# FFN gate and up products as Strassen's seven products of 2x2 blocks (over pairs of f tiles, pairs of k tiles and token halves)

## The chip, the core and the metric

The kernel runs on one core of a Trainium2 chip. The time is that of one execution on the device, in microseconds (us); the time before is the median of 3 runs. In the texts PE is TensorE (its weight loads are PEld), DVE is VectorE, ACT is ScalarE, POOL is GpSimd, and SP is SyncE, on whose queue the kernel issues all its DMAs. L191 is line 191 of the kernel before.

## The reference, cut to what matters

One step of a two-layer streaming encoder in float32. There are T = 640 tokens (512 of one new stream and 8 x 16 of running streams), and each has D = 1024 channels. The stages, in order, are: FFN 0a, the mLSTM and SSD mixer ("ab"), FFN 0b, FFN 1a, the gated DeltaNet mixer ("gdn"), FFN 1b, and a last norm. The change is in the FFNs:

```python
D_MODEL = 1024
D_FF = 2816
def swiglu(x, w_gate, w_up, w_down):
    return (jax.nn.silu(x @ w_gate) * (x @ w_up)) @ w_down
...
    x = x + 0.5 * swiglu(rmsnorm(x, norm_g[l, 0]), ffn_w_gate[l, 0], ffn_w_up[l, 0], ffn_w_down[l, 0])
```

## The kernel before, in words

**Layout.** Activations lie by channels: `self.x[d]`, d = 0..7, is a tile of 128 channels by 640 tokens. A float32 product is made of three float32r products. Both operands are split exactly into a high and a low part, and hi x hi, hi x lo and lo x hi are summed in PSUM (`passes`).

**Activations.** `prep(d)` runs for each channel tile as soon as its residual is written. ACT writes the high part of x times the norm's gain (L273), DVE the low part (L274), and both add the tile's squares to the norm's sum (`sumsq`: ACT L265, DVE L266). The norm's factor itself is needed only behind the products. `rstd` computes it with a small PE product of that sum (L295), a chain of short DVE instructions (L297, L284 to L289), and a second PE product (L307) that spreads it over the partitions as `R` (L308, L309).

**Weights.** `wload` brings [128, 8, 256] of a weight (1 MB) into one of two buffers `wraw` (gate, down and mixer weights) or of two buffers `wraw2` (up weights); line 148 issues the DMA. `split` then works in units of 512 columns: ACT copies the high part (L174), and POOL subtracts it from the weight to give the low part (L175). The results lie in eight buffers `wsp`, so four units (pairs of high and low) can be ready or in use. Splitting has a higher priority in the scheduler than the work around it (`AHEAD` = 300), so it runs as far ahead of PE as `wsp` allows.

**Products.** `mmT` makes one [128 x 640] output in PSUM from 8 k tiles. For each k tile it makes the three passes, and for each pass the two token halves of 320. These are 48 matmuls of 128 x 128 by 128 x 320, all on L191, each with its own weight load. PSUM has two tiles `big` of two banks each, and four tiles `small` of one bank.

**An FFN.** `ffn` goes over 22 f tiles of 128 in three groups, `FF_GROUPS = ((0, 8), (8, 15), (15, 22))`. For each f tile it makes the gate product and the up product, each into one `big`. DVE multiplies each by R (L336), ACT applies silu (L338), DVE multiplies gate by up (L339), and ACT and DVE split the result into h (L341, L342). After each group `wout` adds the group's share of the down product to x. It goes over eight output tiles j, two to each load, and each j takes one `big`; the two alternate, so that the eviction of one (L367, or L365 where the scale is 1) lies beside the products of the other. In the last group of a stage `wout` calls the next stage's `prep` after each j. The last group of FFN 1b goes through `finish` instead (L1701 and behind), which also makes the last norm and writes the output.

**Mixers.** Their projections use `mmT` and `projR` (L386), and their output products use `wout` with two h-like tiles at a time (`out2`, 8 calls in ab and 4 in gdn). Their recurrences are Python generators that advance one step at each `tick`; `mmT` ticks once for each k tile. Where the main stream needs a generator's result, `until` ticks with no main work beside it.

**Order of the work.** The program is written out in full, and a scheduler orders each engine's queue ahead of time by priority and by its own estimate of when inputs are ready. At run time every queue goes in that order.

## Time and profile before

| | |
|---|---|
| time, median of 3 runs (lowest, highest) | 3054.94 us (3054.13, 3055.04) |
| span of the profiled execution | 3055.5 us |
| mean granted TensorE clock | 0.989 |
| PE busy; PEld busy | 2992.0 us; 2889.9 us |
| DVE; ACT; POOL busy | 1219.9; 1090.0; 1038.7 us |
| matmuls on L191, gate, up and mixer projections | 10560 |

A row that groups instructions gives line, engine, operation, written <- read tile, shape, count, then busy time in us, mean ns of one, and the engine's idle time just before them with what ended it. A row of the timeline gives start, length (both in us), engine, line and operation. A row of the windows gives a stretch from:to in us, its length, each engine's busy time with the number of instructions, the granted clock, the DMA share and GB/s. The profiled execution's span is 0.6 us above the median of the runs.

### The profile page before, as it was taken

The page shows a single profiled execution, that of the slowest core. Times are in us where ns is not written, and L with a number is a line of the kernel's source. Part 1 is how long each engine was busy: PE and PEld are TensorE (multiplying, and loading weights), DVE is VectorE, ACT ScalarE, POOL GpSimd, SP SyncE. Part 2 cuts the span into 40 slices and gives each one's busy share as a digit, 9 for nine tenths or more (in the row PEclk, how much of TensorE's full clock was granted, in tenths as well). Part 3 has the DMA queues.
Part 4 walks back from the last instruction along what each step waited for, and adds up shares of the span by engine and source line. Part 5 has one row for each costly group of instructions (what it writes and reads, how often), then busy time and mean ns, then how long its engine had stood idle before and what let it go on. Part 6 is the DMA issues. An engine that isn't in the chain of part 4 may idle for free. (4 is left out here: it accounts for less than half of the span.)

```text
span 3055.5 us, 50975 instructions
## 1 busy us (share of the span) xinstructions
PE 2992.0 (98%) x20870; PEld 2889.9 (95%) x20870; DVE 1219.9 (40%) x2419; ACT 1090.0 (36%) x2385; POOL 1038.7 (34%) x871
## 2 busy tenths in 40 slices
PE   8999999999999999999999999999999999999998
PEld 8999999999988899999999999999888998999998
DVE  4212125233566662121233122236777755212124
ACT  4222234343444342222232222234555454222225
POOL 3333332222223133333333333333323223333334
PEclk9999999999999999999999999999999999999999
DMA  5222213222313232222132222122122213222213
GB/s 149 70 69 66 94 37 83 72 81 88 96 56 91 71 115 70 69 82 78 53 95 70 84 70 74 58 75 61 48 73 56 86 51 108 71 68 82 79 52 107
DMA packets 268159, 233.70 MB, mean 76 GB/s; under 512 B 22103, under 2 KB 266468, under 8 KB 267926
## 3 DMA queue, kind: packets, MB, share of 16 engines
q1 hardware_dynamic: 267926, 230.44, 24.6%
q8 instruction: 165, 2.70, 0.4%
q14 instruction: 68, 0.56, 0.1%
HBM read 211.80 MB, written 18.60 MB: 75 GB/s over the span
## 5 line engine op out<-in xcount | busy, mean ns | idle before, releaser
L175 POOL TENSOR_TENSOR wsp<-wraw,wsp 128x512 fp32r<-128x512 f32 (+2 forms) x808 | 993.4, 1233 | 1970.0 <-ACT wsp L174 1786.3
L191 PE MATMUL big<-xg,wsp 128*128 128x320 f32 x10560 | 1609.3, 310 | 0.9 <-DVE x L252 0.9
L191 PEld LDWEIGHTS big<-xg,wsp 128*128 128x128 f32 x10560 | 1558.0, 188 | 22.5 <-issue 19.7
L174 ACT ACTIVATE wsp<-wraw 128x512 fp32r<-128x512 f32 (+2 forms) x808 | 480.1, 597 | 1292.0 <-PE big L191 1151.8
L191 PE MATMUL big<-h,wsp 128*128 128x320 f32 x3888 | 572.1, 308 | 0.0
L191 PEld LDWEIGHTS big<-h,wsp 128*128 128x128 f32 x3888 | 570.7, 188 | 0.0
L336 DVE TENSOR_TENSOR gu<-big,R 128x640 f32<-128x640 f32 x176 | 145.3, 826 | 817.9 <-PE big L191 817.6
L386 PE MATMUL big<-wsp,xg 128*128 128x256 f32 x1920 | 240.5, 282 | 1.5 <-DVE zs L1680 1.4
L367 DVE SCALAR_TENSOR_TENSOR x<-big,x 128x640 f32<-128x640 f32 x88 | 72.6, 825 | 410.9 <-PE big L191 410.9
L386 PEld LDWEIGHTS big<-wsp,xg 128*128 128x128 f32 x1920 | 229.3, 190 | 4.4 <-DVE zs L1680 2.2
L191 PE MATMUL big<-y,wsp 128*128 128x320 f32 x768 | 130.3, 318 | 5.0 <-DVE x L365 5.0
L339 DVE TENSOR_TENSOR gu<-gu,gu 128x640 f32<-128x640 f32 x88 | 129.7, 1474 | 9.4 <-DVE gu L336 0.5
L191 PEld LDWEIGHTS big<-y,wsp 128*128 128x128 f32 x768 | 114.4, 189 | 16.1 <-issue 14.7
L341 ACT ACTIVATE h<-gu 128x640 fp32r<-128x640 f32 x88 | 65.0, 739 | 179.7 <-DVE gu L339 179.7
L568 DVE SCALAR_TENSOR_TENSOR tmp<-tmp,taps,tmp 128x664 f32<-128x664 f32 x108 | 101.9, 943 | 14.4 <-ACT tmp L562 13.1
L342 DVE TENSOR_TENSOR h<-gu,h 128x640 fp32r<-128x640 f32 x88 | 72.8, 828 | 70.8 <-ACT h L341 70.8
L365 DVE TENSOR_TENSOR x<-big,x 128x640 f32<-128x640 f32 x96 | 78.4, 821 | 49.0 <-PE big L191 48.2
L338 ACT ACTIVATE gu<-gu 128x640 f32<-128x640 f32 x88 | 65.1, 740 | 39.0 <-DVE gu L336 38.9
L191 PE MATMUL big<-yT,wsp 128*128 128x320 f32 x384 | 70.9, 334 | 3.5 <-DVE x L365 2.7
L191 PEld LDWEIGHTS big<-yT,wsp 128*128 128x128 f32 x384 | 60.8, 201 | 10.5 <-issue 5.6
L274 DVE SCALAR_TENSOR_TENSOR xg<-x,gain,xg 128x640 fp32r<-128x640 f32 x48 | 48.8, 1023 | 28.4 <-ACT xg L273 28.3
L1701 PE MATMUL big<-h,wsp 128*128 128x384 f32 (+1 forms) x336 | 54.1, 314 | 0.4 <-DVE h L342 0.2
(426 smaller groups left out, 2089.6 us busy)
## 6 DMA issues: line engine op xcount, KB each, us to landing
wraw<-in_ffn_w_up SPq DMA_DIRECT2D x43, 1024.0 KB
wraw<-in_ffn_w_gate SPq DMA_DIRECT2D x43, 1024.0 KB
wraw<-in_ffn_w_down SPq DMA_DIRECT2D x36, 896.0 KB
wraw<-in_ffn_w_down SPq DMA_DIRECT2D x16, 1024.0 KB
wraw<-in_ab_w_in SPq DMA_DIRECT2D x16, 1024.0 KB
wraw<-in_gdn_w_in SPq DMA_DIRECT2D x16, 1024.0 KB
wraw<-in_ab_w_out SPq DMA_DIRECT2D x32, 256.0 KB
wraw<-in_ab_w_in SPq DMA_DIRECT2D x12, 512.0 KB
```

The costliest lines, as they stand in the source:

```text
L174: nc.scalar.activation(out=hi, in_=src[:, i : i + n], func=AF.Copy)
L175: nc.gpsimd.tensor_tensor(lo, src[:, i : i + n], hi.bitcast(F32), ALU.subtract)
L191: self.nc.tensor.matmul(ps[:, half, :HT], lhsT=wp, rhs=ap[:, half * HT : half * HT + HT], start=(k == 0 and i == 0), stop=(k == n - 1 and ...
L336: nc.vector.tensor_tensor(e.rearrange("p (a b) -> p a b", a=2), ps[:, :, :HT], self.r2(), ALU.mult)
L338: nc.scalar.activation(out=ev[0], in_=ev[0], func=AF.Silu)
L339: nc.vector.tensor_tensor(ev[0], ev[0], ev[1], ALU.mult)
L341: nc.scalar.activation(out=h[:, 0], in_=ev[0], func=AF.Copy)
L342: nc.vector.tensor_tensor(h[:, 1], ev[0], h[:, 0].bitcast(F32), ALU.subtract)
L365: nc.vector.tensor_tensor(xj, ps[:, :, :HT], xj, ALU.add)
L367: nc.vector.scalar_tensor_tensor(xj, ps[:, :, :HT], scale, xj, ALU.mult, ALU.add)
L386: self.nc.tensor.matmul(ps[:, t % 2, :256], lhsT=ap[:, t * P : (t + 1) * P], rhs=wp, start=(k == 0 and i == 0), stop=(k == ND - 1 and i == 2))
L568: nc.vector.scalar_tensor_tensor(y[:, :n], xp[:, k : k + n], taps[:, j, k : k + 1], y[:, :n], ALU.mult, ALU.add)
```

## The change

The gate and up products go over pairs. For two f tiles (columns of the weight), two k tiles and the two token halves, the eight block products are replaced by seven products (Strassen's, in Winograd's form) of sums of weight blocks with sums of activation blocks. One `pair_up` makes the gate (or the up) outputs of two f tiles: seven products, each over 4 pairs of k tiles and three passes. These are 84 matmuls of 128 x 128 by 128 x 320, where two calls of `mmT` made 96.

- **Weights** (`weights7`). Of the seven weight operands three are blocks as loaded and four are sums, made on DVE from 512-column blocks into five buffers `S`. All seven are split by ACT and POOL as before, in units of 512 columns.
- **Activations** (`prep2`, in place of `prep` ahead of an FFN). For every pair of channel tiles it makes the seven activation operands, each split into high and low, partly in buffers shared with the mixers (`ext` "A", "B", "C").
- **Results** (`pair_up`). The seven products are combined from four PSUM banks by DVE. The gate pair uses both `big`, the up pair all four `small`. Some banks are read while their sum is half made, and are added to afterwards.
- **h.** Silu, gate times up, and the split of h work on both f tiles at once (1280 columns).
- **`wout`** goes over two output tiles j together: k outside, j inside, both `big` at once, and one tick per k tile. It splits the weights of two j in one call.
- **Buffers.** `wraw2` has one buffer; h has three of twice the size; several mixer tiles take theirs from `ext`; `finish` takes its output rows from the tiles `xg`.
- **Groups.** `FF_GROUPS` has four groups, the last of six f tiles.

Comments and docstrings, dropped in the diff, are left out below, as are the mixers' lines that only take a tile from `ext`.

```diff
-FF_GROUPS = ((0, 8), (8, 15), (15, 22))
+FF_GROUPS = ((0, 4), (4, 10), (10, 16), (16, 22))
...
+    def ext(self, which, dtype=F32):
+        return lambda tag, shape, bufs=1: self.t(f"ext{which}", shape, {"A": 6, "B": 4, "C": 2}[which], dtype)
...
-        w = tile("wraw2", [P, 2048], bufs=2) if tile else self.t("wraw", [P, 2048], bufs=2)
+        w = tile("wraw2", [P, 2048]) if tile else self.t("wraw", [P, 2048], bufs=2)
...
+    def prep2(self, d, which, total=True):
+        nc = self.nc
+        if total:
+            self.sumsq(d)
+        if d % 2 == 0:
+            return
+        p = d // 2
+        x0, x1 = self.x[d - 1], self.x[d]
...
+        def gained(dst, src, g):
+            nc.scalar.activation(out=dst[:, 0], in_=src, func=AF.Copy, scale=g)
+            nc.vector.scalar_tensor_tensor(dst[:, 1], src, g, dst[:, 0].bitcast(F32), ALU.mult, ALU.subtract)
+        def plain(dst, src):
+            nc.scalar.activation(out=dst[:, 0], in_=src, func=AF.Copy)
+            nc.vector.tensor_tensor(dst[:, 1], src, dst[:, 0].bitcast(F32), ALU.subtract)
+        u, v = self.tmp(), self.tmp()
+        d0, d1, y, s2 = u[:, :HT], u[:, HT:T], v[:, :HT], v[:, HT:T]
+        gained(a[:, :, lo_half], x0[:, lo_half], g0)
+        nc.vector.tensor_tensor(d0, x0[:, hi_half], x0[:, lo_half], ALU.subtract)
+        nc.vector.tensor_tensor(d1, x1[:, lo_half], x1[:, hi_half], ALU.subtract)
+        nc.scalar.activation(out=d0, in_=d0, func=AF.Copy, scale=g0)
+        nc.vector.scalar_tensor_tensor(s2, x1[:, hi_half], g1, d0, ALU.mult, ALU.subtract)
+        plain(t2, s2)
+        plain(t1, d0)
+        nc.scalar.activation(out=y, in_=x0[:, hi_half], func=AF.Copy, scale=g0)
+        nc.vector.scalar_tensor_tensor(y, x1[:, hi_half], g1, y, ALU.mult, ALU.subtract)
+        plain(t3, y)
+        gained(b, x1, g1)
+        nc.vector.scalar_tensor_tensor(d1, d1, g1, d0, ALU.mult, ALU.add)
+        plain(t4, d1)
+        self.xs[p] = (a[:, :, lo_half], t2, t1, t3, b[:, :, lo_half], b[:, :, hi_half], t4)
...
+    def weights7(self, tile, raw):
...
+        def total(x, y, op):
+            s = tile("S", [P, ND // 2, P], bufs=5)
+            with self.tc.high_priority(offset=self.ahead):
+                nc.vector.tensor_tensor(s, x, y, op)
+            return s
+        def parts(src):
+            hi, lo = (self.unit().rearrange("p (a b) -> p a b", b=P) for _ in range(2))
+            with self.tc.high_priority(offset=self.ahead):
+                nc.scalar.activation(out=hi, in_=src, func=AF.Copy)
+                nc.gpsimd.tensor_tensor(lo, src, hi.bitcast(F32), ALU.subtract)
+            return hi, lo
+        yield parts(a11)
+        s1 = total(a21, a22, ALU.add)
+        s2 = total(s1, a11, ALU.subtract)
+        yield parts(s2)
+        yield parts(s1)
+        yield parts(total(a11, a21, ALU.subtract))
+        yield parts(a12)
+        yield parts(total(a12, s2, ALU.subtract))
+        yield parts(a22)
+    def product(self, ps, w, acts, first, last):
+        n = len(acts)
+        for k, a in enumerate(acts):
+            for i, (wp, ap) in enumerate(((w[0], 0), (w[0], 1), (w[1], 0))):
+                self.nc.tensor.matmul(ps, lhsT=wp[:, k], rhs=a[:, ap],
...
+    def pair_up(self, tile, raw, banks):
...
+        b1, b6, b5, b7 = banks
+        w = self.weights7(tile, raw)
+        B = list(zip(*self.xs))
+        self.product(b1, next(w), B[0], True, False)
+        self.product(b6, next(w), B[1], True, True)
+        nc.scalar.copy(u, b1)
+        nc.vector.tensor_tensor(u, b6, u, ALU.add)
+        self.product(b5, next(w), B[2], True, False)
+        nc.vector.tensor_tensor(v, b5, u, ALU.add)
+        self.product(b7, next(w), B[3], True, False)
+        nc.vector.tensor_tensor(c22, b7, v, ALU.add)
+        self.product(b1, next(w), B[4], False, True)
+        nc.vector.tensor_tensor(c11, b1, self.R[:, :HT], ALU.mult)
+        self.product(b5, next(w), B[5], False, True)
+        nc.vector.tensor_tensor(c12, b5, u, ALU.add)
+        self.product(b7, next(w), B[6], False, True)
+        nc.vector.tensor_tensor(c21, b7, u, ALU.add)
+        nc.vector.tensor_tensor(c12, c12, self.R[:, HT:], ALU.mult)
+        nc.vector.tensor_tensor(g[:, T:], g[:, T:], self.R, ALU.mult)
+        return g
...
-            for f in range(g0, g1):
+            for f in range(g0, g1, 2):
...
-                for n in ("g", "u"):
-                    w = self.split(raw[n][:, :, c : c + P], ND, P)
-                    ps = self.big()
-                    self.mmT(ps, w, self.xg)
-                    e = tile("gu", [P, T], bufs=4)
-                    nc.vector.tensor_tensor(e.rearrange("p (a b) -> p a b", a=2), ps[:, :, :HT], self.r2(), ALU.mult)
-                    ev.append(e)
+                ev = [self.pair_up(tile, r, self.banks(i == 0)) for i, r in enumerate(raw)]
                 nc.scalar.activation(out=ev[0], in_=ev[0], func=AF.Silu)
                 nc.vector.tensor_tensor(ev[0], ev[0], ev[1], ALU.mult)
...
         for jb in range(4):
             raw = self.wload(w[:, :, jb * 256 : jb * 256 + 256], n, 256)
-            for j in (2 * jb, 2 * jb + 1):
-                c = (j % 2) * P
-                wj = self.split(raw[:, :, c : c + P], n, P)
-                ps = self.big()
-                self.mmT(ps, wj, acts)
+            wj = self.split(raw, n, 256)
+            pss = [self.big(), self.big()]
+            for k, a in enumerate(acts):
+                for c, ps in enumerate(pss):
+                    for i, (wp, ap) in enumerate(self.passes(wj[k], a)):
+                        for half in range(2):
+                            nc.tensor.matmul(
...
+                self.tick()
+            for c, ps in enumerate(pss):
+                j = 2 * jb + c
...
-            return lambda d, total=True: self.prep(d, 3 * l + {"a": 0, "b": 2}.get(s, 1), total)
+            prep = self.prep2 if kind == "ffn" else self.prep
+            return lambda d, total=True: prep(d, 3 * l + {"a": 0, "b": 2}.get(s, 1), total)
```

More of the change, by code (lines that the diff above doesn't have):

```diff
@@ new lines, in product @@
+    def product(self, ps, w, acts, first, last):
+        n = len(acts)
+        for k, a in enumerate(acts):
+            for i, (wp, ap) in enumerate(((w[0], 0), (w[0], 1), (w[1], 0))):
+                self.nc.tensor.matmul(
+                    ps,
+                    lhsT=wp[:, k],
+                    rhs=a[:, ap],
+                    start=(first and k == 0 and i == 0),
+                    stop=(last and k == n - 1 and i == 2),
+                    skip_group_check=True,
+                )
@@ new lines, in banks @@
+    def banks(self, whole):
+        if whole:
+            a, b = self.big(), self.big()
+            return a[:, 0, :HT], a[:, 1, :HT], b[:, 0, :HT], b[:, 1, :HT]
+        return tuple(self.small()[:, :HT] for _ in range(4))
+    def pair_up(self, tile, raw, banks):
+        nc = self.nc
+        g = tile("G", [P, 2 * T], bufs=2)
+        c11, c12, c21, c22 = (g[:, i * HT : i * HT + HT] for i in range(4))
+        uv = tile("uv", [P, 2, HT], bufs=2)
+        u, v = uv[:, 0], uv[:, 1]
+        b1, b6, b5, b7 = banks
[18 more added lines that the diff above has]
+        return g
@@ L1040, in ssd_post @@
         yield
-        CB = tile("CB", [P, T])
+        CB = self.ext("C")("CB", [P, T])
         for a, b, ps in parts:
@@ L1687, in finish @@
         n = len(acts)
-        pairs = [tile("wraw2", [P, 2048], bufs=2) for _ in range(2)]
-        yrows = [w2[:, a : a + 1024] for w2 in pairs for a in (0, 1024)] + [tile("yrow", [P, 1024])]
+        yrows = [self.t(f"xg{t}", [P, 1024]) for t in range(NT)]
         for ts in (range(0, 3), range(3, NT)):
```

59 lines of the change are left out of this document (36 added, 23 removed).

## The prediction

> **What bounds the kernel now.** I read the page first (engine shares, then the costliest groups).
>
> ```profile
> span 3055.5 us, 50975 instructions
> PE 2992.0 (98%) x20870; PEld 2889.9 (95%) x20870; DVE 1219.9 (40%) x2419; ACT 1090.0 (36%) x2385; POOL 1038.7 (34%) x871
> L191 PE MATMUL big<-xg,wsp 128*128 128x320 f32 x10560 | 1609.3, 310 | 0.9 <-DVE x L252 0.9
> L191 PEld LDWEIGHTS big<-xg,wsp 128*128 128x128 f32 x10560 | 1558.0, 188 | 22.5 <-issue 19.7
> L175 POOL TENSOR_TENSOR wsp<-wraw,wsp 128x512 fp32r<-128x512 f32 (+2 forms) x808 | 993.4, 1233 | 1970.0 <-ACT wsp L174 1786.3
> L174 ACT ACTIVATE wsp<-wraw 128x512 fp32r<-128x512 f32 (+2 forms) x808 | 480.1, 597 | 1292.0 <-PE big L191 1151.8
> ```
>
> PE is busy 98% of the span, and everyone waits for it: POOL for ACT's high part, ACT for PE to free a weight buffer. So a matmul less is time less, as long as the others keep up. There are as many weight loads as matmuls, so a product per weight costs no extra loads. Next, the timeline inside FFN 0a, where it repeats:
>
> ```profile
> 69.66 0.83 DVE L336 TENSOR_TENSOR gu<-big,R 128x640 f32<-128x640 f32 x1 [6.22 <-PE big L191]
> 70.14 1.29 POOL L175 TENSOR_TENSOR wsp<-wraw,wsp 128x512 fp32r<-128x512 f32 x1 [2.23 <-ACT wsp L174]
> 70.59 1.52 DVE L339 TENSOR_TENSOR gu<-gu,gu 128x640 f32<-128x640 f32 x1
> 72.92 0.82 DVE L342 TENSOR_TENSOR h<-gu,h 128x640 fp32r<-128x640 f32 x1 [0.81 <-ACT h L341]
> 83.74 0.82 DVE L336 TENSOR_TENSOR gu<-big,R 128x640 f32<-128x640 f32 x1 [6.21 <-PE big L191]
> 84.22 1.29 POOL L175 TENSOR_TENSOR wsp<-wraw,wsp 128x512 fp32r<-128x512 f32 x1 [2.25 <-ACT wsp L174]
> ```
>
> One f tile (gate and up, 96 matmuls) lasts 83.74 - 69.66 = 14.08 us, 146.7 ns for a matmul. The second thing to see: L339 has two inputs in SBUF and began while POOL worked. It ended at 72.11, which is 0.68 after POOL's end at 71.43: it waited for POOL and then ran its 640 columns. L342, with POOL idle, took 0.82. L336 reads PSUM and one SBUF tile; it overlaps POOL at 84.22 and neither is longer. Two more places:
>
> ```profile
> 9.32 2.52 POOL L175 TENSOR_TENSOR wsp<-wraw,wsp 128x512 fp32r<-128x512 f32 x2 [6.56 <-ACT wsp L174]
> 2575.99 0.17 DVE L287 TENSOR_TENSOR nr<-nr 128x5 f32<-128x5 f32 x1
> 2576.16 1.31 POOL L175 TENSOR_TENSOR wsp<-wraw,wsp 128x512 fp32r<-128x512 f32 x1 [4.50 <-ACT wsp L174]
> 2576.20 1.29 DVE L288 TENSOR_TENSOR nr<-nr 128x5 f32<-128x5 f32 x1
> ```
>
> Five columns took 1.29 us instead of 0.17 because POOL had begun. So POOL's subtraction and a DVE instruction with two SBUF inputs exclude each other. Back to back POOL needs 1.26 for a unit.
>
> The stage joints, from the windows (the start, then inside an FFN, then the joints ab to FFN 0b and gdn to FFN 1b):
>
> ```profile
> 0.00:18.00 18.00, 8.48 (x41) 6.60 (x41) 11.38 (x24) 10.32 (x16) 4.59 (x13) 1.00 0.91 263
> 60.00:500.00 440.00, 440.00 (x3010) 439.42 (x3009) 113.19 (x132) 120.94 (x191) 162.03 (x131) 1.00 0.23 73
> 1100.00:1131.00 31.00, 25.55 (x161) 24.33 (x160) 24.81 (x35) 16.14 (x26) 11.94 (x10) 0.94 0.49 146
> 2551.00:2580.00 29.00, 24.19 (x162) 22.86 (x162) 23.80 (x36) 16.50 (x27) 12.24 (x10) 1.00 0.51 157
> ```
>
> At a joint PE is idle 5 us and DVE is busy for over 80%: there DVE sets the pace.
>
> **The change part by part.**
>
> *Matmuls.* Gate and up have 4 x 22 x 2 x 48 = 8448; pairs make 4 x 11 x 2 x 84 = 7392. 1056 x 0.1467 = **-154.9**. A `pair_up` then lasts 12.32 us on PE instead of 14.08.
>
> *Splitting and DVE beside the products.* Per `pair_up`: POOL seven units (before four). DVE four sums of 512, the R products of 320 and 640, and half of two 1280-column instructions, all with two SBUF inputs; besides six 320-column evictions from PSUM. For the evictions:
>
> ```profile
> L553 DVE TENSOR_TENSOR tmp<-big,R 128x320 f32<-128x320 f32 x36 | 17.5, 487 | 24.8 <-PE big L191 24.3
> ```
>
> What excludes each other, at best: DVE at 0.68 for 640 gives 4 x 0.54 + 0.34 + 0.68 + 1.36 = 4.5; with POOL 7 x 1.2 (1.29 less a tenth for starting) = 8.4, 12.9 us. At worst, whole profiled lengths: 7 x 1.30 + 4 x 0.69 + 0.49 + 0.82 + 1.5 = 14.7. Both exceed PE's 12.32. But four `wsp` units are ready when a group begins, worth 4 x 12 x 0.1467 = 7.0 us. A group of six `pair_up`s loses 6(p - 12.32) - 7.0 for a period p, one of four 4(p - 12.32) - 7.0, nothing below zero. I take the middle, p = 13.85: 6.5 + 0, over three groups of six in each of four FFNs about **+26** (ends 0 and 95). ACT's seven units take 7 x 0.60 = 4.2 us (L174's mean), hidden.
>
> A DVE instruction that waits for POOL holds up whatever is queued behind it: the next sums, on which ACT and POOL wait, and the evictions. PE waits for two of these inside a pair: the sixth product goes into the bank that DVE must have read after the third, the seventh into the one read after the fourth. Both lie two products (24 matmuls, 3.5 us) ahead, so an ordinary lock of 1.3 us is covered, two or three in a row are not; that is rival 1's way to PE.
>
> The Trainium skill (SBUF — State Buffer, Who interferes with whom) speaks against this change: a VectorE instruction with two SBUF inputs contends with a GpSimd one that reads SBUF, as an exclusive lock held for the whole instruction. The rows agree (0.68 after POOL's end). Were the two only slowed a little, this term would be 0 and the sum about 3004.
>
> *Joints ahead of an FFN.* `prep2` replaces `prep`; the prices:
>
> ```profile
> 1102.01 0.89 DVE L274 SCALAR_TENSOR_TENSOR xg<-x,gain,xg 128x640 fp32r<-128x640 f32 x1 [0.90 <-ACT xg L273]
> 1102.81 0.82 DVE L365 TENSOR_TENSOR x<-big,x 128x640 f32<-128x640 f32 x1
> 1105.54 0.82 DVE L266 TENSOR_TENSOR tmp<-tmp,tmp 128x640 f32<-128x640 f32 x1
> ```
>
> A pair of channel tiles cost DVE 2 x (0.82 + 0.89 + 0.82) = 5.06. It now costs two evictions and two sums (3.28), ten instructions of 320 at 0.487 and one of 640: 9.04. Four pairs: +16 us, on the engine that sets the pace. PE's cover (the first products of the pairs at hand) is about as large as before. Two joints behind mixers: +32. FFN 0b to 1a: `wout` gives PE 72 x 0.1467 = 10.6 for a pair, so only the last pair shows, 9.04 less 36 ready matmuls (5.3): +4. At the start, `prep2` adds as much, but there the loads rule as well (the first window: DMA share 0.91), and PE can begin with the pairs that have come: +6 (0 to 16). Ahead of a mixer the last two output tiles now end together, one more `prep` of 2.53 at two joints: +5. Together **+47** (20 to 75; the upper end adds POOL's locks).
>
> *Group ends.*
>
> ```profile
> L341 ACT ACTIVATE h<-gu 128x640 fp32r<-128x640 f32 x88 | 65.0, 739 | 179.7 <-DVE gu L339 179.7
> L1701 PE MATMUL big<-h,wsp 128*128 128x384 f32 (+1 forms) x336 | 54.1, 314 | 0.4 <-DVE h L342 0.2
> ```
>
> The last h comes after an eviction (0.49), the R product (0.82), gate times up on 1280 columns (2 x 0.68 and a tenth: 1.5), ACT's copy (below 2 x 0.74: 1.4) and the low part (1.5): 5.7, or up to 9.3 with a lock at each of three DVE steps; I take 7.5. Cover: `wout` over the h tiles at hand, four in a group of six (48 matmuls, 7.0), two in the first group (3.5), in `finish` 12 matmuls (at L1701's 54.1/336 = 0.16: 1.9). 11 x 0.5 + 4 x 4.0 + 5.5 = **+27** (10 to 55).
>
> *`wout` on both banks.* The first bank ends six matmuls (0.88) before the second and its eviction takes 0.82: nothing is lost if DVE is free. It was busy 40% of the time; with half a microsecond left of what it does, 0.2 for each of 93 changes of load (45 in FFNs, 48 in mixers): **+19** (0 to 90). Before, the two `big` alternated and this wait was small (first of two rows of PE's waits; then one of SP's):
>
> ```profile
> PE big L191 <- DVE x L365: 7.6, 7, 2.1
> PE small L1004 <- DVE y L998: 2.1, 2, 1.9
> SPq L148 <- POOL wsp L175: 2240.2, 208, 27.7
> ```
>
> *Ticks.* `out2` gives 8 ticks instead of 16. Counting steps in the code, only the end of ab is short: the last quad and its norm need 35 ticks, of which two `out2` gave 32 and now 16. The three ticks without cover are the second row's place (2.1): 16 more by 0 to 0.7, **+6** (0 to 11).
>
> *Shared buffers.* The mixers' tiles now share `ext` buffers, with as many for each kind as before or more, but a tile can wait for another kind's reader. PE hardly waits for such tiles now (its longest waits for a background step are some 2 us, second row above), so there is next to nothing to gain: 0, with an upper end at five such waits, 10.
>
> *Loads.* With one `wraw2` the next up load waits until the last is split, and gate and down loads are queued behind it on SP. Loads waited for buffers before (third row, up to 27.7) and PE did not. 1 MB at the 146 GB/s of the 1100 stretch takes 7.2 us, and the gate pair before it 12.32: 0; without that cover it would be up to 7 for each up pair.
>
> *Clock.* The 1100 stretch was granted 0.94: 1.9 us lost where PE paused. More pauses at three joints: **+5** (0 to 15). The Trainium skill (TensorE: Matmul & The Clock Gate, Part 1) has the clock halve after an idle window of about 3.4 us; by it as an estimate each long pause costs some 2 us more, which agrees with the 0.94.
>
> Sum: 3055.5 - 154.9 + 26 + 47 + 27 + 19 + 6 + 5 = 3030.6; less the 0.6 by which the profiled execution lies above the median: **3030**.
>
> **The rivals.**
>
> 1. *POOL and DVE shut each other out and become the bound* (slower). Place: inside the gate and up products; price: p = 14.7, +95 instead of +26, **3099**. Without this term the sum is 3004, so it is slower by 0.2% from 57 us on: 12 x (6d - 7) + 4 x (4d - 7) = 57, d = 1.92, p = 14.2. For it: both sums exceed 12.32, and DVE's own work (4.5 + 2.9 + starting) leaves little room for waiting. Against: the 7 us in hand, and POOL idle two thirds of the time before.
> 2. *DVE's queue holds PE at the banks* (slower). 0.75 for each change of load: +70 instead of +19, **3081**. For it: mixers' DVE work; against: the 7.6 us above.
> 3. *All covers hold.* Joints +20, the rest +10: 3055 - 155 + 30 = **2930**. For it: the scheduler fills PE's queue with whatever is ready.
> 4. *The gain is just eaten up*: between 3049 and 3061.
>
> That the change does not remove the matmuls can't be: the code counts them.
>
> **How the numbers follow.** Chances: forecast 0.42, rival 1 0.22, rival 2 0.14, rival 3 0.13, rival 4 0.09. 0.2% (6 us) is about what a measurement of this kernel can tell from no change. Faster by more: 0.42 + 0.13 = 0.55; same 0.09; slower 0.36. Taking the terms' ends as independent, the root of the squares gives 47 below and 107 above: 2983 to 3137. The low end goes out to 2950 for part of rival 3, and the high end stays at 3130. Within the forecast alone: 2960 to 3049.
>
> **What would show it.** The matmuls of gate and up fall by 1056. Where an FFN repeats, the distance of two `pair_up`s: near 12.3 if PE still binds, 14 and more for rival 1, with POOL's units well over 1.3 us and PE waiting for POOL. PE's waits for L365 and L367 over 50 us would be rival 2. At the joints 1100 and 2551, DVE busy some 16 us longer. At group ends, PE waiting for h 0 to 6 us. The forecast is wrong if the FFNs' repeating part is slower than 13.9, or a wait for DMA shows in PE's chain.

## The result, and the profile after

The changed kernel takes 3274.20 us (median of four runs, 3269.37 to 3277.80) where the kernel before takes 3054.99 (3054.13 to 3058.39): the ratio is 1.0714, 95% interval 1.0699 to 1.0729. It is slower, by 219 us; 3030 had been predicted. The profiled run took 3272.64 us, 2.0 more than its span.

The page and, by tile and shape, the groups of the changed kernel (busy us, mean ns of one | idle time before them and what ended it):

```profile
span 3270.6 us, 50977 instructions
PE 2956.7 (90%) x19814; PEld 2811.5 (86%) x19814; DVE 1856.9 (57%) x3387; ACT 1271.9 (39%) x2683; POOL 1501.3 (46%) x1075
L401 PE MATMUL big<-xg,wsp 128*128 128x320 f32 x2112 | 384.6, 334 | 191.2 <-DVE uv L429 131.3
L383 POOL TENSOR_TENSOR wsp<-S,wsp 128x512 fp32r<-128x512 f32 x352 | 533.6, 1517 | 312.9 <-ACT wsp L382 309.5
L376 DVE TENSOR_TENSOR S<-wraw 128x512 f32<-128x512 f32 x176 | 164.7, 936 | 122.9 <-POOL wsp L383 61.8 <-DMA wraw<-in_ffn_w_gate 47.6 <-DMA wraw<-in_ffn_w_up 13.3
L376 DVE TENSOR_TENSOR S<-wraw,S 128x512 f32<-128x512 f32 x88 | 116.6, 1325 | 41.4 <-POOL wsp L383 41.4
```

The 1056 matmuls are gone (20870 to 19814). What replaced them is idle time and slower matmuls. PE's busy time fell by 35 us only (2992.0 to 2956.7), where 1056 x 0.1467 = 155 is what the matmuls alone were worth, so those that are left take 120 us more; and PE's idle time grew from 63.5 to 313.9 us. Of the products' matmuls (L401) only those into `big` wait, which are the gate pairs; the largest releaser is DVE's u (L429), the first of the sums that a `pair_up` makes from its banks. A sum of weights (L376) takes up to 1325 ns on average, POOL's unit (L383) 1517.

The waits (us in total, times, longest):

```profile
PE big L401 <- DVE uv L429: 131.3, 31, 6.2
PE big L401 <- DVE G L437: 30.0, 27, 2.2
DVE S L376 <- POOL wsp L383: 200.9, 122, 4.9
```

The windows of the changed kernel: inside FFN 0a as in the prediction, then one group of six `pair_up`s of FFN 0b and the `wout` behind it.

```profile
60.00:500.00 440.00, 396.12 (x2546) 387.38 (x2545) 228.50 (x293) 144.81 (x228) 259.22 (x179) 0.95 0.21 66
1299.00:1390.00 91.00, 79.99 (x509) 78.22 (x508) 50.76 (x70) 34.09 (x54) 61.55 (x42) 0.94 0.20 64
1390.00:1433.00 43.00, 42.71 (x288) 41.90 (x286) 16.44 (x18) 8.60 (x14) 17.84 (x13) 1.00 0.27 86
```

Before, the first window had 3010 matmuls at a clock of 1.00; now it has 2546 at 0.95. Neither DVE (52%) nor POOL (59%) is near full. `wout` runs at PE's pace (288 matmuls in 43 us); the loss sits in the products. From the first to the last of its 504 matmuls a group of six `pair_up`s takes 90.6 us (mean of the twelve groups in the trace), where 504 x 0.1467 = 73.9.

The timeline shows where it goes. Two f tiles (an f pair) take a gate `pair_up` and an up `pair_up`, the gate pair and the up pair below. First DVE, then PE, at the turn from an up pair to the next f pair's gate pair:

```profile
1358.69 0.69 DVE L376 TENSOR_TENSOR S<-wraw 128x512 f32<-128x512 f32 x1 [1.05 <-DMA wraw<-in_ffn_w_up]
1359.49 1.59 DVE L376 TENSOR_TENSOR S<-S,wraw 128x512 f32<-128x512 f32 x1
1361.00 1.79 DVE L376 TENSOR_TENSOR S<-wraw 128x512 f32<-128x512 f32 x1
1362.72 1.77 DVE L376 TENSOR_TENSOR S<-wraw,S 128x512 f32<-128x512 f32 x1
1364.41 0.48 DVE L439 TENSOR_TENSOR G<-small,uv 128x320 f32<-128x320 f32 x1
1364.92 0.82 DVE L441 TENSOR_TENSOR G<-G,R 128x640 f32<-128x640 f32 x1
1365.78 1.49 DVE L460 TENSOR_TENSOR G<-G,G 128x1280 f32<-128x1280 f32 x1
1367.19 0.48 DVE L429 TENSOR_TENSOR uv<-big,uv 128x320 f32<-128x320 f32 x1
```

```profile
1358.18 1.92 PE L401 MATMUL big<-xg,wsp 128*128 128x320 f32 x12
1362.58 1.04 PE L401 MATMUL big<-extB,wsp 128*128 128x320 f32 x6
1367.73 1.70 PE L401 MATMUL big<-xg,wsp 128*128 128x320 f32 x5 [4.11 <-DVE uv L429]
1367.80:1372.30 4.50, 4.50 (x17) 4.50 (x18) 1.96 (x2) 1.29 (x2) 2.09 (x1) 0.50 0.00 0
```

PE begins the gate pair at 1358.18, finishes its third product at 1363.62 and stands for 4.11 us. DVE meanwhile makes the four sums of the up pair, which PE needs only a whole pair later; they come first in its queue. The first waited for the up load, the next three were lengthened from 0.69 to 1.6-1.8 by POOL's units. Behind them stand the last eviction of the old up pair (its matmuls ended about 1358.3), the R product, gate times up, and only then u. PE's next five matmuls take 1.70 us, about double: the stop also cost half the clock for a while (last row, one of the windows: a granted clock of 0.50 in the 4.5 us behind it). A group of six has two such turns, a group of four one, 28 in all; the view of the waits counts 31 waits for u of 4.2 us on average, these 28 and three at joints.

In the built program the fifth product's first matmul carries a wait for L429 in a gate pair (bank 0 of a `big` tile, whose bank 1 L429 reads), and the fourth one for L431; in an up pair, whose four banks are four `small` tiles, the fifth waits only for ACT's copy (L428). In PE's queue some matmuls of a gate pair's fifth product (five in the turn above) stand ahead of the fourth, so that PE needs u as soon as the third product is done. The trace agrees: all 31 waits for L429 are waits of `big`.

### The profile page after: what moved, and what is told of

It is laid out like the page before. It is cut to its first block, busy times and chain, and to the rows that moved or that the text cites. A ratio compares the mean times of both kernels' runs of the same rounds, so it can differ in the third digit from the quotient of the medians.

```text
span 3270.6 us, 50977 instructions
## 1 busy us (share of the span) xinstructions
PE 2956.7 (90%) x19814; PEld 2811.5 (86%) x19814; DVE 1856.9 (57%) x3387; ACT 1271.9 (39%) x2683; POOL 1501.3 (46%) x1075
## 4 chain that ended last, share of the span: by engine, by line
PE 42%; DVE 13%; issue 3%; POOL 2%; DMA 2%; ACT 2%; POOLq 0%; DVEq 0%; ACTq 0%; SPq 0%
PE big L486 14%; PE small L401 10%; PE big L401 9%; DVE S L376 4%; PE big L196 3%; POOL wsp L383 2%; DMA wraw<-in_ffn_w_up 2%; PE big L1833 1%; PE big L519 1%; DVE tmp L701 1%; DVE G L460 1%; PE small L1709 1%; DVE G L441 1%; DVE UB L1572 1%; DVE subst L1569 1%
## 5 line engine op out<-in xcount | busy, mean ns | idle before, releaser
L180 POOL TENSOR_TENSOR wsp<-wraw,wsp 128x512 fp32r<-128x512 f32 (+1 forms) x396 | 550.3, 1396 | 1048.0 <-ACT wsp L179 816.4
L383 POOL TENSOR_TENSOR wsp<-S,wsp 128x512 fp32r<-128x512 f32 x352 | 533.6, 1517 | 312.9 <-ACT wsp L382 309.5
L401 PE MATMUL big<-xg,wsp 128*128 128x320 f32 x2112 | 384.6, 334 | 191.2 <-DVE uv L429 131.3
L383 POOL TENSOR_TENSOR wsp<-wraw,wsp 128x512 fp32r<-128x512 f32 x264 | 379.0, 1436 | 361.3 <-ACT wsp L382 281.3
L401 PEld LDWEIGHTS big<-xg,wsp 128*128 128x128 f32 x2112 | 345.0, 205 | 213.8 <-DVE uv L429 139.7
L179 ACT ACTIVATE wsp<-wraw 128x512 fp32r<-128x512 f32 (+1 forms) x396 | 245.8, 623 | 526.9 <-PE big L486 299.3
L382 ACT ACTIVATE wsp<-S 128x512 fp32r<-128x512 f32 x352 | 221.1, 630 | 449.9 <-PE big L401 249.2
L196 PE MATMUL big<-xg,wsp 128*128 128x320 f32 x2112 | 369.9, 320 | 0.0
L196 PEld LDWEIGHTS big<-xg,wsp 128*128 128x128 f32 x2112 | 316.8, 190 | 26.7 <-issue 25.2
L401 PE MATMUL small<-xg,wsp 128*128 128x320 f32 x2112 | 331.4, 308 | 0.0
L401 PEld LDWEIGHTS small<-xg,wsp 128*128 128x128 f32 x2112 | 316.0, 188 | 0.0
L382 ACT ACTIVATE wsp<-wraw 128x512 fp32r<-128x512 f32 x264 | 166.4, 630 | 344.0 <-PE big L401 98.3
L376 DVE TENSOR_TENSOR S<-wraw 128x512 f32<-128x512 f32 x176 | 164.7, 936 | 122.9 <-POOL wsp L383 61.8
L500 DVE SCALAR_TENSOR_TENSOR x<-big,x 128x640 f32<-128x640 f32 x120 | 98.9, 824 | 190.8 <-PE big L486 187.3
L401 PE MATMUL big<-extA,wsp 128*128 128x320 f32 x792 | 166.2, 353 | 20.3 <-ACT wsp L382 8.6
L401 PEld LDWEIGHTS big<-extA,wsp 128*128 128x128 f32 x792 | 147.1, 226 | 25.3 <-DVE uv L431 9.7
L376 DVE TENSOR_TENSOR S<-S,wraw 128x512 f32<-128x512 f32 x88 | 98.5, 1119 | 102.2 <-POOL wsp L383 97.8
L376 DVE TENSOR_TENSOR S<-wraw,S 128x512 f32<-128x512 f32 x88 | 116.6, 1325 | 41.4 <-POOL wsp L383 41.4
```

The costliest lines, as they stand in the source:

```text
L179: nc.scalar.activation(out=hi, in_=src[:, i : i + n], func=AF.Copy)
L180: nc.gpsimd.tensor_tensor(lo, src[:, i : i + n], hi.bitcast(F32), ALU.subtract)
L196: self.nc.tensor.matmul(ps[:, half, :HT], lhsT=wp, rhs=ap[:, half * HT : half * HT + HT], start=(k == 0 and i == 0), stop=(k == n - 1 and ...
L376: nc.vector.tensor_tensor(s, x, y, op)
L382: nc.scalar.activation(out=hi, in_=src, func=AF.Copy)
L383: nc.gpsimd.tensor_tensor(lo, src, hi.bitcast(F32), ALU.subtract)
```

## The experiments

Two theories grew out of this. **Rate** (X in the expectations, Q in the first ones): POOL and DVE exclude each other for so long that a pair can't be fed in 12.3 us, wherever PE then stands. **Burst** (B; its parts at first as T, the tied banks, O, the queue's order, L, the late load): there is enough time in a pair, but at the turn so much stands ahead of u in DVE's queue that PE's three products run out. All edits are to the changed kernel. Ratios are to runs of the kernel before that were made beside each run (medians 3052 to 3058 us). In the table "group" is the mean length of a group of six `pair_up`s, PE's own pace being 73.9; "u" is PE's wait for u in total, in us. Line numbers shift by a few between the runs: a product's matmul is L398 to L408, u L426 to L433, a sum L375 to L383.

| run | us | ratio to before, 95% | group | u |
|---|---|---|---|---|
| the change | 3274 | 1.071 (1.070-1.073) | 90.6 | 131 |
| e1_untied | 3177 | 1.039 (1.036-1.042) | 84.5 | 103 |
| e2_order | 3245 | 1.062 (1.059-1.065) | 88.9 | 112 |
| e3_order_untied | 3166 | 1.036 (1.033-1.039) | 83.2 | 96 |
| e4_low_on_act | 3058 | 1.000 (0.999-1.001) | 77.1 | 31 |
| e5_loads3 | 3303 | 1.083 (1.079-1.088) | 93.3 | 154 |
| e6_untied_loads3 | 3218 | 1.055 (1.051-1.060) | 87.4 | 103 |
| e7_dvelow | 3047 | 0.997 (0.996-0.999) | 75.4 | 11 |
| e8_dvelow_order | 3033 | 0.994 (0.992-0.996) | 75.4 | 9 |
| e9_dvelow_alone | 3197 | 1.047 (1.043-1.050) | 89.1 | 117 |
| e10_no_loads3 | 3061 | 1.002 (1.000-1.003) | 77.5 | 26 |
| e11_no_sums | 3079 | 1.008 (1.005-1.010) | 79.4 | 66 |
| e12_two_lows | 3115 | 1.020 (1.016-1.024) | 79.9 | 58 |
| e13_sums_behind | 3173 | 1.038 (1.035-1.041) | 85.0 | 83 |
| e14_gu_late | 3256 | 1.065 (1.061-1.070) | 91.5 | 95 |
| e15_sums_gu | 3090 | 1.011 (1.008-1.014) | 79.2 | 4 |
| e16_all | 3034 | 0.993 (0.990-0.995) | 74.7 | 9 |
| e17_all_order | 3027 | 0.990 (0.988-0.992) | 75.6 | 0 |
| e18_joint_lows | 3032 | 0.991 (0.989-0.994) | 74.7 | 7 |

**e1_untied.** Tied banks.

```
 def banks(self, whole):
-    if whole:
-        a, b = self.big(), self.big()
-        return a[:, 0, :HT], a[:, 1, :HT], b[:, 0, :HT], b[:, 1, :HT]
-    return tuple(self.small()[:, :HT] for _ in range(4))
+    a = self.big()
+    return a[:, 0, :HT], a[:, 1, :HT], self.small()[:, :HT], self.small()[:, :HT]
```

> The products' banks are dealt out anew: the first and second product of every pair (gate and up alike) share a two-bank tile, the third and fourth have one-bank tiles of their own. Now the fourth product no longer waits for DVE to read the third's bank, and the fifth waits for DVE's read of the second's bank with two products between. Theory T (the tile ties two banks, so PE waits for DVE's queue with no product between): the 31 waits of PE for DVE's u (131 us) fall below 40, the half-clock stretches behind them go too, and the time falls from 3274 by 130 to 190, to 3085 to 3145. Rival Q (DVE and POOL together need some 15 us per pair, and where PE waits doesn't matter): the waits move to POOL's and ACT's weights and the time stays at 3230 to 3285.

97 us faster, less than T said. The first and second product still share a tile, and the fifth still waits for u; but PE now gets through four products before it needs u. The same turn, DVE and then PE:

```profile
1423.16 0.72 DVE L376 TENSOR_TENSOR S<-wraw 128x512 f32<-128x512 f32 x1 [2.44 <-DMA wraw<-in_ffn_w_up]
1430.70 0.48 DVE L427 TENSOR_TENSOR uv<-big,uv 128x320 f32<-128x320 f32 x1
1431.24 3.39 PE L401 MATMUL big<-xg,wsp 128*128 128x320 f32 x12 [2.82 <-DVE uv L427]
```

A wait for u is 2.3 us on average instead of 4.2, about one product's cover (1.76 us) less, though there are 44 instead of 31. The 36 us of waits for L431 and for c12 (L437, tied in the same way) shrink to 2, and the granted clock rises from 0.957 to 0.966. What stands in DVE's queue at the turn is the same.

**e2_order** and **e3_order_untied.** The sums without priority, alone and with the banks.

```
-            with self.tc.high_priority(offset=self.ahead):
-                nc.vector.tensor_tensor(s, x, y, op)
+            nc.vector.tensor_tensor(s, x, y, op)
```

> Only DVE's four sums of weights lose their high priority, so they are queued behind the evictions of the pair before instead of ahead of them. Rival O (the order of DVE's queue is the cause): u is read as soon as the second product is done, the waits of PE for u fall from 131 us to below 40 and the time to 3100 to 3170, though sums that come late make PE wait for weights. Theory T: the tie remains, the fourth product still waits for a step of DVE that directly follows the third, but the steps are nearer: 3180 to 3260. Rival Q (DVE and POOL together are the bound): no gain, 3250 to 3330.

> Both edits at once: banks dealt out anew and the sums without priority. If T and O are two halves of one cause, the time is lowest here, 3050 to 3120, and lower than either alone by 30 or more. If T alone is the cause, it is within 20 of the first run. If Q is right, it stays above 3230.

Only 29 and, beyond the banks, 11 us. That does not speak against the order. At the turn all four sums still stand ahead of u, two of them ahead of the last eviction: the scheduler orders by its own estimate of what is ready first. The edit did not make the order it was meant to make.

**e4_low_on_act.** No POOL beside the products; the subtraction of the low parts is left out.

```
-                nc.gpsimd.tensor_tensor(lo, src, hi.bitcast(F32), ALU.subtract)
+                nc.scalar.activation(out=lo, in_=src, func=AF.Copy)
```

> The low parts of the gate and up weights are copied by ACT instead of being subtracted by POOL (the subtraction of the high part is left out, so this part of the computation is changed): POOL does nothing beside the gate and up products, and nothing excludes DVE there. ACT makes 14 units of about 0.6 us in a pair instead of 7. Rival Q or a lock theory (POOL's units lengthen DVE's sums from 0.69 to 1.3 and that makes u late): the sums take 0.7, the waits for u fall from 131 us to below 40, a pair lasts 12.5 to 13, and the time is 3040 to 3110. Theory T without the lock: the sums still stand ahead of u (four times 0.7 us), the waits fall by half at most, 3130 to 3190. If neither: above 3230.

216 us faster, with the ties, the order and the loads of the change. Its sums, by shape:

```profile
L376 DVE TENSOR_TENSOR S<-wraw 128x512 f32<-128x512 f32 x176 | 130.1, 739 | 135.9 <-ACT wsp L383 79.3 <-DMA wraw<-in_ffn_w_gate 46.0 <-DMA wraw<-in_ffn_w_up 3.0
L376 DVE TENSOR_TENSOR S<-wraw,S 128x512 f32<-128x512 f32 x88 | 60.3, 686 | 1.7 <-ACT wsp L383 0.4
```

The third kind of sum takes 686 ns instead of 1325. A turn, the first of the four sums, then u, then PE:

```profile
179.08 0.69 DVE L376 TENSOR_TENSOR S<-wraw 128x512 f32<-128x512 f32 x1 [0.18 <-DMA wraw<-in_ffn_w_up]
184.55 0.49 DVE L429 TENSOR_TENSOR uv<-big,uv 128x320 f32<-128x320 f32 x1
185.10 0.85 PE L401 MATMUL big<-xg,wsp 128*128 128x320 f32 x4 [0.22 <-DVE uv L429]
```

Between the first two rows stand the same instructions in the same order as in the change; they take 5.5 us instead of 8.5, and PE waits 0.22 us instead of 4.11. Without the lock the same queue is short enough at the turn; this run alone can't say whether rate or burst was cured.

**e5_loads3** and **e6_untied_loads3.** Three load buffers in turn for gate and up.

```
-        w = tile("wraw2", [P, 2048]) if tile else self.t("wraw", [P, 2048], bufs=2)
+        if tile:
+            self.loads += 1
+        w = tile("wraw2", [P, 2048]) if tile and self.loads % 3 == 2 else self.t("wraw", [P, 2048], bufs=2)
...
-for w, tl in ((wg, None), (wu, tile))]
+for w, tl in ((wg, tile), (wu, tile))]
```

> Only the load buffers change: gate and up weights take three buffers in turn (two of them still shared with the down weights) instead of gate two and up one, so an up load may be issued one pair earlier; the space is the same. Theory L (the load into the single up buffer is issued only when POOL has split the last of the up weights, DVE's first sum waits for it, and evictions stand behind that sum): the waits of DVE's sums for loads fall from 61 us to below 15, u comes 1 to 2 us earlier in every second pair, and the time falls from 3274 by 40 to 90. If POOL's and DVE's exclusion alone sets the pace: below 20 of change.

> Three load buffers and the banks dealt out anew (3177 with the banks alone). Theory L: in that run DVE stood 2.4 us in a pair for the up load with two evictions ready behind the sum; without it two pairs last 26 instead of 28.2 us, and the time is 3080 to 3120. If exclusion sets the pace (a pair of 14.1 us in every order): 3160 to 3185.

Theory L falls: 29 and 40 us slower than without. The sums' waits for loads don't fall in total (61 us in the change, 67 in e5), but those that are left lie beside `wout` and at the joints. At the turn DVE no longer stands for the up load, and uses the time otherwise (e5):

```profile
1370.16 1.79 DVE L379 TENSOR_TENSOR S<-wraw,S 128x512 f32<-128x512 f32 x1
1371.88 2.57 DVE L463 TENSOR_TENSOR G<-G,G 128x1280 f32<-128x1280 f32 x1
1374.37 0.68 DVE L379 TENSOR_TENSOR S<-wraw 128x512 f32<-128x512 f32 x1
1375.78 1.49 DVE L467 TENSOR_TENSOR h<-G,h 128x1280 fp32r<-128x1280 f32 x1 [0.73 <-ACT h L466]
1377.19 0.48 DVE L432 TENSOR_TENSOR uv<-big,uv 128x320 f32<-128x320 f32 x1
```

Gate times up is lengthened to 2.57 us, a sum of the next pair and the low part of h, with its wait for ACT, now stand ahead of u as well, and PE waits 5.26 us there. The late load had been one filler of the queue; something else takes the place.

**e7_dvelow** and **e8_dvelow_order.** As e6, with four of seven low parts on DVE; then also the sums without priority.

```
-                nc.gpsimd.tensor_tensor(lo, src, hi.bitcast(F32), ALU.subtract)
+                (nc.vector if dve else nc.gpsimd).tensor_tensor(lo, src, hi.bitcast(F32), ALU.subtract)
...
-        yield parts(s2)
+        yield parts(s2, True)
```

(and so for the other three summed weights).

> As the run before with one change more: the low parts of the four summed weights are subtracted by DVE instead of POOL, which keeps three of seven. A unit takes DVE about 0.69 us where POOL takes 1.29, so what excludes each other falls to 8 x 0.69 + 3 x 1.29 + 2.5 = 11.9 us, less than PE's 12.3. Exclusion theory: a pair lasts 12.4 to 13.0 and the time is 3010 to 3070, 40 or more below the run before. Rival (DVE's own queue is the bound, with 8 x 0.69 + 2.9 + 2.5 = 10.9 us of work and every wait in order): no gain or a loss against the run before.

> As the run before, with DVE's sums without priority, so that evictions stand ahead of them. If the order in DVE's queue still costs PE anything after the other three edits, it is 10 to 40 below the run before; if not, sums that come late cost 0 to 20.

Both as expected: 75.4 us a group is about 2% from PE's pace. e8 is 14 us below e7, so the order still cost something, but most of the gain came with POOL's units. This pointed to Rate, and the next run was to prove it.

**e9_dvelow_alone**, **e10_no_loads3** and **e12_two_lows.** e9 is e7's move of the low parts without the other edits, e10 is e8 without the three buffers, and e12 is e10 with two low parts on DVE instead of four.

> The change as it is, banks, priorities and loads included, with one edit: DVE instead of POOL subtracts the low parts of the four summed weights. Theory X (POOL's units and DVE's two-input instructions exclude each other and need more than PE's 12.3 us a pair; tie, order and loads only pass DVE's lag on to PE): this one edit takes nearly all of it, 3030 to 3070, with a group of six pairs at 75 to 78 us instead of 90.4. Theory T (the tied banks are a cause of their own): PE still waits for u and v, 3090 to 3150, a group at 80 to 84.

> Banks dealt out anew, sums without priority, four low parts on DVE, and the change's own load buffers (two and one). If three load buffers cost 29 to 40 us of themselves (as they did where POOL made all the low parts), this is 3000 to 3015; if they cost only because sums came still further ahead of the evictions, it is within 8 of the same kernel with three buffers, 3025 to 3041.

> As the second run of this call, but DVE makes only two of the four low parts and POOL five of seven. With POOL making all seven a pair took 13.8 us in this order (83 us for a group of six), with three of seven 12.5 (75.2). Theory X: two units moved save 2 x (1.29 - 0.69) = 1.2 us of exclusion, so a group takes 76 to 78 us and the time is 3040 to 3080. If what matters is that a low part follows its sum on the same engine, half the effect: a group at 79, 3085 to 3110.

e9 and e10 miss both ranges. e12 does too, but 3115 us and a group of 79.9 lie near the second's 3085 to 3110 and 79. In e9 the exclusion of a pair falls by 4 x (1.29 - 0.69) = 2.4 us, and a group still takes 89.1 us: Rate alone can't be the cause. Its turn:

```profile
1328.09 1.80 DVE L376 TENSOR_TENSOR S<-wraw,S 128x512 f32<-128x512 f32 x1
1331.67 2.55 DVE L460 TENSOR_TENSOR G<-G,G 128x1280 f32<-128x1280 f32 x1
1334.14 0.48 DVE L429 TENSOR_TENSOR uv<-big,uv 128x320 f32<-128x320 f32 x1
1334.67 1.21 PE L401 MATMUL big<-xg,wsp 128*128 128x320 f32 x4 [4.16 <-DVE uv L429]
```

Three POOL units a pair are enough to lengthen the sum and gate times up in this place, and two low parts of DVE (1.3 us) have joined the queue there. In e10 three buffers would have been worth 28 us (e8 against it), where they cost 29 and 40 in e5 and e6: what a buffer is worth hangs on what else stands at the turn. With banks dealt out and no priority, none, two and four low parts on DVE give 3166, 3115 and 3061 us (e3, e12, e10): half the move, half the effect.

**e11_no_sums.** The sums are left out; the products take unsummed weights.

```
         def total(x, y, op):
-            s = tile("S", [P, ND // 2, P], bufs=5)
-            with self.tc.high_priority(offset=self.ahead):
-                nc.vector.tensor_tensor(s, x, y, op)
-            return s
+            return x
```

> The change as it is without DVE's four sums of weights (left out: the products take unsummed weights in their place); POOL still subtracts seven low parts a pair. Theory X: what excludes each other falls to 7 x 1.25 + 2.5 = 11.3 us, below PE's 12.3, so a group of six pairs takes 74 to 78 us and the time is 3010 to 3060. If POOL's seven units behind ACT are too slow by themselves, a group stays above 84 and the time above 3130.

19 us above the range, and the group, 79.4, is above its 78. PE waits for none of POOL's seven units, so they can be made in time; with the sums gone u is still late by 66 us in all, since gate times up and h remain ahead of it.

**e13_sums_behind**, **e14_gu_late**, **e15_sums_gu.** Burst against Rate: the work, POOL's units, the ties and the buffers as in the change, only DVE's order fixed by hand; the sums behind c22 of the pair before; gate times up and the low part of h behind u and v of the next gate pair; both.

```
+        self.behind = nc.vector.tensor_tensor(c22, b7, v, ALU.add).ins
...
-            with self.tc.high_priority(offset=self.ahead):
+            with self.tc.high_priority(offset=self.ahead), self.tc.issue_after(behind):
                 nc.vector.tensor_tensor(s, x, y, op)
```

```
+        done = nc.vector.tensor_tensor(v, b5, u, ALU.add)
+        if self.late:
+            with self.tc.issue_after(done.ins):
+                self.late()
```

(`late` holds the silu, gate times up and h of the f pair before.)

> The change as it is, but each pair's four sums of weights are queued on DVE behind the last bank read that the pair before needs for its own products (c22), so none stands between the end of an up pair and the u of the next gate pair. In that stretch are left the last eviction, the R product, gate times up (2.5 us with the lock), and the low part of h, which stands ahead of u here and waits 1.3 us for ACT: about 0.5 + 1.4 + 2.5 + 1.3 + 1.5 + 0.5 = 7.7 us against 5.3 us of three products. Theory B (what costs is the burst in DVE's queue at the turn from up to gate, once in two pairs, against three products): PE's wait for u falls from 4.1 to about 2.4 us, the time to 3150 to 3200. Theory X (POOL and DVE together need 13.8 us a pair or more in any order): a group of six pairs stays above 84 us and the time above 3190.

> The change as it is, but gate times up of two pairs and the low part of h are queued on DVE behind u and v of the next gate pair. The four sums stay where they are. Theory B: the 2.5 us of gate times up leave the stretch, so PE's wait for u falls from 4.1 to 1 to 2 us, the time to 3130 to 3190, and c22 comes later without holding PE. Theory X: a group stays above 84 us and the time above 3190.

> Both of the moves before it at once; tied banks, POOL's seven low parts and the load buffers are those of the change. The stretch is left with the last eviction, the R product and u, 2.4 us even with a lock, under the 5.3 us of three products. Theory B: PE's wait for u goes, a group of six pairs takes 74 to 78 us, the time is 3040 to 3090. Theory X: the time that POOL and DVE exclude each other remains and a group takes 82 us or more, the time is above 3150.

e13's time and waits are as Burst said (2.7 us a wait, 82.5 in 31); its group, 85.0, is just above Rate's 84. e14 misses Burst's range and lies in Rate's: with gate times up gone the four sums, led by a wait of 1.88 for the up load and three of them lengthened to 1.3-1.8, hold u by themselves, PE still waits 3.6 at such a turn, and its waits for c12 rise from 30 to 44 us in all. Each of these two moves half of what stands ahead of u; e15, which moves both, decides. With no instruction less on any engine it is 184 us faster than the change. The time is at the upper end of Burst's range, and the group, 79.2, lies between Burst's 78 and Rate's 82, nearer to the first. Its turn, DVE and PE:

```profile
155.32 0.48 DVE L447 TENSOR_TENSOR G<-small,uv 128x320 f32<-128x320 f32 x1
155.83 1.40 DVE L449 TENSOR_TENSOR G<-G,R 128x640 f32<-128x640 f32 x1
159.53 0.49 DVE L431 TENSOR_TENSOR uv<-big,uv 128x320 f32<-128x320 f32 x1 [2.31 <-ACT uv L430]
160.42 0.49 DVE L433 TENSOR_TENSOR uv<-big,uv 128x320 f32<-128x320 f32 x1 [0.39 <-PE big L405]
160.83 1.48 DVE L461 TENSOR_TENSOR G<-G,G 128x1280 f32<-128x1280 f32 x1
```

```profile
154.94 1.92 PE L405 MATMUL big<-xg,wsp 128*128 128x320 f32 x12
160.22 0.89 PE L405 MATMUL big<-xg,wsp 128*128 128x320 f32 x5
```

DVE is idle before u, and PE, which began the pair at 154.94, begins the fifth product without a gap; its five matmuls take 0.89 us, not 1.70. The lock has not gone: POOL's units for these products take 960 us in all (913 in the change), DVE's sums 326 (380). They now meet where PE needs nothing from DVE at once. So the stop takes both, the order and the lock: without the lock the old order costs little (e4), and with it the new order does. What is left of Rate in this order (waits, then the window of the prediction):

```profile
PE small L405 <- POOL wsp L387: 43.7, 55, 1.3
60.00:500.00 440.00, 423.88 (x2830) 413.51 (x2829) 240.08 (x320) 160.93 (x256) 290.37 (x194) 1.00 0.24 76
```

In the up pairs PE waits for POOL's units, 0.8 us each time, which follow sums that now come late. The clock is back at 1.00. So of the 16.7 us that a group had lost, 11.4 go with the order of DVE's queue alone (90.6 to 79.2; it also moves where locks fall); of the other 5.3, the banks, buffers and low parts of e16 take 4.5.

**e16_all** and **e17_all_order.** The two moves with untied banks, three buffers and four low parts on DVE; then the sums also without priority.

> Both moves, the banks dealt out anew, three load buffers, and four low parts on DVE. The products ran at PE's pace already without the moves (75.2 us a group of six, 3033 to 3047 in all), so what is left lies at the joints and the start. Theory B and X alike: 3020 to 3045.

> As the run with all the edits (3034), with DVE's sums without priority. Inside the FFNs PE already runs at its own pace, 74.7 us a group of six, so only the stretches ahead of an FFN can answer: there eight sums no longer stand in front of the last channel pair's steps, but the first pair's sums come late. Same as before the edit within 8 us, 3025 to 3042.

e17 has the lowest median: 3027 us, 0.990 of the kernel before (0.988-0.992), so both beat the kernel before and the change. That 3027 lies near the 3030 of the prediction bears nothing out: other banks, buffers and low parts made it. In e17 PE waits for u nowhere; the window of the prediction:

```profile
60.00:500.00 440.00, 434.09 (x2914) 425.94 (x2913) 293.28 (x433) 163.23 (x269) 170.71 (x113) 1.00 0.25 80
```

**e18_joint_lows.**

```
         def plain(dst, src):
             nc.scalar.activation(out=dst[:, 0], in_=src, func=AF.Copy)
-            nc.vector.tensor_tensor(dst[:, 1], src, dst[:, 0].bitcast(F32), ALU.subtract)
+            nc.scalar.activation(out=dst[:, 1], in_=src, func=AF.Copy)
```

> As the run with all the edits (3034), but the four plain low parts of each channel pair's activations ahead of an FFN are copied by ACT instead of subtracted by DVE (the subtraction is left out, so this part of the computation is changed). DVE does 4 x 0.41 = 1.6 us less of 8.0 for a channel pair, ACT 1.9 more. If DVE's work sets the pace of the joints, each of the two behind a mixer is 5 to 6.5 us shorter, the start 2 to 6, the turn from 0b to 1a about 1.6: 3012 to 3022. If the loads, the half clock or ACT set it, it stays within 5: 3029 to 3039.

Inconclusive. The profiled run was at 3019, in the first range; the other three lie between 3030 and 3037, and the median, 3032, can't be told from e16. Whether DVE's work alone sets the joints' price stays open.

## Why the prediction was wrong

**The step that failed** is "Splitting and DVE beside the products": +26, at most 95. By its own formula, 12 x (6(p - 12.32) - 7.0) + 4 x (4(p - 12.32) - 7.0), the twelve groups' 90.6 us (15.1 a pair, where 13.9 had been named as the sign of being wrong) give p = 16.3 (6 x 3.95 - 7.0 = 16.7) and a term of about 235: 200 measured in the groups of six, and 35 by the formula for the groups of four. p had been bounded at 14.7, the sum of all lengths that exclude each other. As a bound on a rate that was sound: e15 does all of that work in 79.2 / 6 = 13.2 us a pair. What failed is that it is not a rate that PE meets. Two statements carried it. One was that the two reads for which PE waits inside a pair "lie two products (24 matmuls, 3.5 us) ahead": in a gate pair the fourth product already waits for DVE's read after the third, and the fifth for the read after the second, because two banks share a tile (e1: 97 us). The other, that "an ordinary lock of 1.3 us is covered, two or three in a row are not", was left to rival 1 and not followed into the order of DVE's queue: at every turn there stand four sums, two end steps of the old pair and gate times up, 5.6 us without locks (4 x 0.69 + 0.48 + 0.82 + 1.49) and 8.5 with them (1358.69 to 1367.19), against 5.3 us of three products. The prediction had the parts of that sum, but added them over a pair and never set them in one place.

**Rival 1** had the right engines, the right way to PE (locked DVE instructions that hold up evictions) and the right sign, and, at 3099, too small a price. One of its marks did not show: in the products PE waited 131 us for DVE's u and only 5.7 for POOL. **Rivals 2 and 3** are wrong: PE's waits for the evictions of `wout` (L498 and L500) come to 46.5 us, under rival 2's 50, of which 23.4 are two waits at joints and only 5.2 lie at `wout` inside the FFNs; and the covers did not hold. One slip of the sums: the terms' lower ends give a root of 46, not 47; nothing hangs on it.

**The clock**, +5 (0 to 15), is the second mis-sized term: granted 0.957 instead of 0.989, 0.043 x 3270.6 - 0.011 x 3055.5 = 107 us at full clock. It is no separate loss but what every stop at a turn brings with it, and lies within the 235 and the joints. Behind the stop shown above, 17 matmuls took 4.69 us (1367.73 to 1372.42) instead of 17 x 0.1467 = 2.49, 2.2 more. The number of pauses, 31 at u alone, was not foreseen. The Trainium skill (TensorE: Matmul & The Clock Gate, Part 1) had been cited for an estimate of some 2 us more for each long pause, and this stop agrees; the idle window of about 3.4 us that it names is longer than many pauses that cost the clock here (last section).

**The lock** itself was read rightly: with POOL off beside the products, the sums fall from 1325 to 686 ns. The rule of the Trainium skill (SBUF — State Buffer, Who interferes with whom) is borne out by that.

**Right in size.** Matmuls: 1056 fewer. Group ends, +27: behind the first group of each FFN 192 matmuls of `wout` take 35.4 us instead of 28.2, 4 x 7.2 = 29; behind the groups of six next to nothing. `wout` on both banks: 43.45 us for 288 matmuls instead of 42.25, 0.3 for each of four changes of load where 0.2 was taken.

**Joints**, +47 with the mixers' shares of `wout` and ticks beside it: the R copy of FFN 0a comes at 59.3 instead of 38.5 us, 20.8 later (+6 was taken), ab is 25.7 longer, gdn 17.3, and FFN 0b loses 21 more than FFN 0a. That is 85 against some 63. Most of the 21 lies at the turn from FFN 0b to 1a, for which +4 was taken: from the last `wout` to R it now takes 26 us (1700.9 to 1727.1) instead of 8.4, and PE waits there for split weights, for the norm's sum and for u (1.5 to 3.6 us each). At the joint behind ab the windows show DVE as the prediction had it:

```profile
1160.00:1210.00 50.00, 28.45 (x150) 26.65 (x149) 44.23 (x82) 25.36 (x49) 11.23 (x7) 0.80 0.17 53
```

DVE is busy 88% of it and the clock is 0.80. Together 235 + 85 + 29 + 14 (the change of loads in twelve groups) = 363 of the 370 us that lie between the span and 3055.5 - 154.9. FFN 0a by itself fits too: from its R to the next it takes 31.9 us more than before, where a quarter of the matmuls' 154.9 (38.7) should have gone, so 70.6 are to be explained; 3 x 16.7 + 8.8 + 7.3 + 3.6 (groups of six, group of four, its end, loads) = 69.8.

**Loads.** "a wait for DMA shows in PE's chain" was named as a mark of failure, and the chain does hold 2% for the up load; e5, where no turn waits for it and the time is 29 us longer, shows that it was not the cause.

## What to carry to other kernels

When a change gives an in-order engine more work beside a busy one, don't only add the work up against the period: write its queue down in order at the place where the busy engine next needs a result, add the lengths with their locks, and set them against what the busy engine can do until then. Check in the built program for what unit (bank or whole tile) a wait is taken. When an edit that "should" fix the order moves the time little, look whether it changed the order at all (e2), and fix the order itself (e15) before concluding that there is too much work.

## What the runs showed of the hardware

Pauses of PE of little more than 2 us can cost the clock. In e14 a pause of 2.11 us was followed by twelve matmuls at nearly half speed:

```profile
182.95 3.54 PE L401 MATMUL big<-xg,wsp 128*128 128x320 f32 x12 [2.11 <-DVE G L441]
197.35 1.92 PE L401 MATMUL big<-xg,wsp 128*128 128x320 f32 x12
```

Counted in that trace are the pauses of PE that began at the full clock. Of those of 2.0 to 2.6 us, 16 of 21 were followed within 2 us by a stretch at half the clock, of those of 2.6 to 3.3 us 13 of 15, but of those of 0.3 to 1.2 us 4 of 59. And the lock of POOL and DVE adds up where DVE's two-input instructions come in a row beside POOL: the sum at 1359.49 and the two behind it took 1.59, 1.79 and 1.77 us, where the same sums without POOL (e4) take 0.69 each.
